# Softmax weights scaled on POOL ahead of P V, and an attention output kept with features on partitions

## The chip, the cores and the metric

One core of a Trainium2 chip runs the kernel. The metric is the device time of one execution in microseconds. The kernel before took 651.96 us as the median of 3 runs (651.56 to 653.12).

## The reference, cut to what matters

One decoder layer on 512 tokens of 1024 features, in float32. Two groups of eight heads with 64 output features each work side by side, and each group's output is normalised before a shared output projection:

```python
p = exp(s - m);  p = p / max(sum(p), 1e-30)          # masked softmax
y_mla = p_mla @ v                                    # 8 heads, causal
y_nsa = g0 * (p_c @ v_cmp) + g1 * (p_s @ v_slc) + g2 * (p_w @ v_win)   # g: sigmoid gates
mixed = concat(rmsnorm(y_mla, g_out_mla), rmsnorm(y_nsa, g_out_nsa))
h = h + mixed @ w_o
h = h + relu(rmsnorm(h) @ w_up) ** 2 @ w_down        # then a final rmsnorm
```

With 512 tokens, all 8 selected blocks are taken and the window is 512, so the selected branch and the window branch are both plain causal attention over four blocks of 128 tokens. The compressed branch attends to 31 (padded to 32) compressed keys.

## The kernel before, in words

A float32 operand that enters a matmul is split in two float32r parts, a high part (a rounded copy, by ACT) and a low part (the difference, by DVE); a product is the sum of two or three matmuls. Values V stand as a 128-column stationary tile: 64 columns of high parts beside 64 of low parts. So P V, with the transposed weights as the moving operand, comes out with features on partitions, 64 rows of the high product over 64 of the low one (`ot`, 128 x 512), and the two halves are still to be added.

The attention stretch is a pipeline of 24 units (`units`, L849): eight MLA heads (`unit_mla`, L654; one head, all four blocks of queries), then eight units of the selected branch and eight of the window and compressed branches (`unit_nsa`, L526, `br` 0 and 1; one block `i` of 128 queries and one group `g` of four heads, in the order of `ORDER`). Each unit has a stage of scores (score matmuls, a DVE operation that masks and finds the limit, an exponential on ACT that also sums) and a stage of P V (L574 on, and L687 on): transposes of the weights on TensorE, the split, two matmuls per block. In step `s` of the loop at L879 the scores of unit `s-1` and the P V of unit `s-2` advance in turn, and `fill` (L862) lets other work advance between the parts: projections that later units need, the compression MLP (`compressed`, L709) and the MLA half of the output projection (`out_mla`, L822). The tile framework then plans one order per engine by a simulated timeline, in which an instruction that stands earlier in the program goes first among those that are ready. Engines run their own queue strictly in order. The weights of a unit live in tiles `pr`, of which there are eight (two units' worth), and `load_wo` (L786) prepares the output weights, three of four times on POOL (`WOENG`, L28).

Behind P V, the kernel before does the following:

- MLA, and blocks 2 and 3 of the selected branch (`add_heads`, L631, `apart`): ACT copies `ot` to SBUF, TensorE transposes it back in four (L642), so that tokens are on partitions; DVE multiplies by the factor per token and head (L644), and POOL adds the halves (L646).
- Blocks 0 and 1 of the selected branch: four f32 matmuls with a folding matrix (`K_FOLD`, L649) transpose and add the halves at once; DVE multiplies (L651). An f32 matmul shows as two instructions in the trace.
- The window branch (L617 on): the same four folds (L623) and an f32 matmul of the transposed compressed weights (L577) with a block diagonal of the compressed values (`vbd`, L621) into one bank; DVE multiplies all by the factors (L626), POOL adds both products to y (L629).
- The factor is 1 / (sum x gate term), `weights_of` (L512): two small DVE operations.
- In units with more than one block, the first block's split goes through SBUF: ACT copies, DVE makes the high part (L591), POOL the low part (L592).
- y has tokens on partitions, so `norm_y` (L779) sums squares along rows on ACT, and `transpose_y` (L802) turns y by four transposes for each block of tokens and half (L805) before it is split and enters `out_proj` (L808).

Of the kernel before, what the change touches and what calls it, by code (L numbers as in the profile page):

```python
# [10 lines left out]
F32 = mybir.dt.float32  # L11
# [6 lines left out]
P = 128  # L18
# [6 lines left out]
APART = lambda br, i: br == -1 or br == 0 and i >= 2  # L25
LOP = lambda br, i, j: j == 0 and i > 0
# [11 lines left out]
DIRECT = lambda br, i: False  # L38
# [39 lines left out]
K_FOLD = 1185  # L78
K_END = 1249
# [15 lines left out]
def layer(ctx, tc, x, xt, w_in, w_uq, w_ukv, w1k, w2k, w1v, w2v, w_o, w_up, w_down, g_final, consts, vecs, out):  # L95
# [430 lines left out]
    def unit_nsa(i, g, br):  # L526
# [36 lines left out]
        if br == 1:  # L563
            nc.gpsimd.tensor_tensor(pc, pc, cm.unsqueeze(2).to_broadcast([P, 4, 32]), op=ALU.subtract)
            nc.scalar.activation(pc, pc, AF.Exp, scale=-1.0)
            if CSUM == "V":
                nc.vector.tensor_reduce(sums[:, 0:4], pc, axis=AX.X, op=ALU.add)
            else:
                half = m["wk2"].tile([P, 4, 16], F32, tag="half", name="half", bufs=2)
                nc.gpsimd.tensor_tensor(half, pc[:, :, 0:16], pc[:, :, 16:32], op=ALU.add)  # L570
                for n in (8, 4, 2):
                    nc.gpsimd.tensor_tensor(half[:, :, 0:n], half[:, :, 0:n], half[:, :, n:2 * n], op=ALU.add)
                nc.gpsimd.tensor_tensor(sums[:, 0:4], half[:, :, 0], half[:, :, 1], op=ALU.add)
        yield "ready"  # L574
# [5 lines left out]
        ot = bank(turn("ot", OT), "ot_ps")  # L580
        phs = []
        for j in range(i + 1):
# [12 lines left out]
            if not DIRECT(br, i):  # L595
                nc.tensor.matmul(ot, vc[:, 4 * j + brg, :], ph, start=(j == 0), stop=False)  # L596
                nc.tensor.matmul(ot, vc[:, 4 * j + brg, :], pl, start=False, stop=(j == i))
            phs.append((ph, pl))
            if j < i or not DIRECT(br, i):
                yield "part"  # L600
        if DIRECT(br, i):

            for h in range(4):
                hs = slice(h * P, (h + 1) * P)
                for j in range(i + 1):
                    for n in range(2):
                        nc.tensor.matmul(ot[:, hs], phs[j][n][:, hs], vc[:, 4 * j + brg, :],
                                         start=(j == 0 and n == 0), stop=(j == i and n == 1))
            yield "part"
        yv = m["yn"][:, i, 256 * g:256 * g + 256].rearrange("p (h d) -> p h d", h=4)  # L610
        gate = sg[:, i, :].rearrange("p (b n) -> p b n", b=3)[:, :, 4 * g:4 * g + 4]
        sv = sums.rearrange("p (b n) -> p b n", b=2)
        if br == 0:
            r = weights_of(sv[:, 1], gate[:, 1], "rg")
            add_heads(ot, r, yv, "direct" if DIRECT(br, i) else APART(br, i))
            return
        r = weights_of(sv, gate[:, 0:3:2], "rg")  # L617
        os_ = wk.tile([P, 512], F32, tag="os", name="os", bufs=2)
        nc.scalar.copy(os_, ot)
        b = bank(turn("ot", OT), "o_ps")  # L620
        nc.tensor.matmul(b[:, 0:256], pct, vbd[g], start=True, stop=True)  # L621
        for h in range(4):
            nc.tensor.matmul(b[:, 256 + 64 * h:320 + 64 * h], os_[:, h * P:(h + 1) * P], cst[:, K_FOLD:K_FOLD + 64],  # L623
                             start=True, stop=True)
        ow = m["wk2"].tile([P, 2, 4, 64], F32, tag="ow", name="ow", bufs=2)
        nc.vector.tensor_tensor(ow.rearrange("p b h d -> p (b h) d"), b.rearrange("p (h d) -> p h d", h=8),  # L626
                                r.rearrange("p b n -> p (b n)").unsqueeze(2).to_broadcast([P, 8, 64]), op=ALU.mult)
        for n in range(2):
            nc.gpsimd.tensor_tensor(yv, yv, ow[:, n], op=ALU.add)  # L629

    def add_heads(ot, r, yv, apart):  # L631

        if apart == "direct":
            b = ot
        else:
            os_ = wk.tile([P, 512], F32, tag="os", name="os", bufs=2)
            nc.scalar.copy(os_, ot)
            b = bank(turn("ot", OT), "o_ps")
        if apart:
            for h in range(4):  # L640
                if apart != "direct":
                    nc.tensor.transpose(b[:, h * P:(h + 1) * P], os_[:, h * P:(h + 1) * P], ident)  # L642
            oa = wk.tile([P, 4, 2, 64], F32, tag="oa", name="oa", bufs=1)
            nc.vector.tensor_tensor(oa.rearrange("p h a d -> p h (a d)"), b.rearrange("p (h n) -> p h n", h=4),  # L644
# [615 lines left out]
```

## Time and profile before

| | |
|---|---|
| median of 3 runs | 651.96 us |
| the profiled execution, its time and its span | 652.88 us, 651.0 us |
| busy: TensorE matmuls, weight loads | 635.2 us (98%), 571.5 us (88%) |
| busy: DVE, ACT, POOL | 429.9 us (66%), 336.6 us (52%), 240.0 us (37%) |
| mean granted clock of TensorE | 0.997 |

Busy time is the union of an engine's instructions. Matmuls overlap in the array and their ends are modelled, so a matmul of 512 columns shows some 390 ns while the next one starts after some 230; the chain of waits counts each piece only as far as it delays the next. The part from 309 us to the end of the span is the MLP.

### The profile page before, as it was taken

Reading aid. Unit: us, or ns where it says so; the run is one execution under the profiler, and the core shown is the slowest. Engines: PE = TensorE matmul, PEld = TensorE weight load, DVE = VectorE, ACT = ScalarE, POOL = GpSimd, SP = SyncE. Lnnn points to the kernel's source line nnn. Section 1 sums busy time; section 2 is a strip of 40 time slices with the busy share of each in tenths; the row PEclk is TensorE's granted clock in tenths of the full one; section 3 lists DMA queues with packets and bytes.
Section 4 is the critical chain, followed back from the end, with each engine's and each line's share of the span. In section 5 each row is a group of like instructions: output and inputs, shape, how many; then the busy total and the mean of one; then the engine's idle time right before and its main releaser. Section 6 shows DMA issues by size and latency. Waiting matters only on the chain.

```text
span 651.0 us, 10981 instructions
## 1 busy us (share of the span) xinstructions
PE 635.2 (98%) x4092; PEld 571.5 (88%) x4092; DVE 429.9 (66%) x898; ACT 336.6 (52%) x702; POOL 240.0 (37%) x294
## 2 busy tenths in 40 slices
PE   7999999999999999999999999999999999999996
PEld 5989999998878888889998889988899988999885
DVE  5767577856788589768967435794259843497425
ACT  5567677857946478732884115541144521355213
POOL 3864402235783139613110225413154231344031
PEclk9999999999999999999999999999999999999998
DMA  6533210105322101063135313254122541124003
GB/s 193 154 99 82 68 50 17 33 2 195 99 78 88 33 2 33 1 216 108 46 116 163 98 33 98 88 171 131 33 81 63 181 140 55 63 68 147 15 2 129
DMA packets 47125, 56.53 MB, mean 87 GB/s; under 512 B 4320, under 2 KB 34784, under 8 KB 47072
## 3 DMA queue, kind: packets, MB, share of 16 engines
q1 hardware_dynamic: 46784, 55.57, 27.9%
q8 instruction: 32, 0.52, 0.3%
q10 hardware_dynamic: 288, 0.26, 0.1%
q14 instruction: 21, 0.17, 0.1%
HBM read 53.72 MB, written 2.10 MB: 86 GB/s over the span
## 4 chain that ended last, share of the span: by engine, by line
PE 86%; DVE 5%; DMA 3%; ACT 2%; POOL 2%; issue 1%; SPq 1%; POOLq 0%; ACTq 0%; DVEq 0%
PE up_ps L990 25%; PE dn_ps L131 9%; PE dn_ps L132 9%; PE dn_ps L130 9%; PE wo_ps L130 2%; PE wo_ps L132 2%; PE wo_ps L131 2%; PE pt_ps L585 2%; PE hid_ps L730 2%; PE s_ps L547 1%; PE pt_ps L692 1%; PE ot_ps L596 1%; PE wq_ps L132 1%; PE wq_ps L131 1%; PE wq_ps L130 1%; PE s_ps L548 1%
## 5 line engine op out<-in xcount | busy, mean ns | idle before, releaser
L130 PE MATMUL dn_ps<-dw,ah 128*128 128x512 f32 (+1 forms) x264 | 101.9, 386 | 0.0
L131 PE MATMUL dn_ps<-dw,ah 128*128 128x512 f32 (+1 forms) x264 | 101.9, 386 | 0.0
L132 PE MATMUL dn_ps<-dw,al 128*128 128x512 f32 (+1 forms) x264 | 101.7, 386 | 0.0
L990 PE MATMUL up_ps<-ttT,uw 128*128 128x256 f32 x720 | 89.5, 282 | 0.4
L990 PEld LDWEIGHTS up_ps<-ttT,uw 128*128 128x128 f32 x720 | 87.2, 189 | 1.0 <-ACT snap L1019 1.0
L990 PE MATMUL up_ps<-ttB,uw 128*128 128x256 f32 x648 | 82.0, 282 | 0.0
L990 PEld LDWEIGHTS up_ps<-ttB,uw 128*128 128x128 f32 x648 | 79.6, 189 | 0.5
L958 POOL TENSOR_TENSOR us<-us,ur 128x1024 f32<-128x1024 f32 x14 | 41.4, 2958 | 101.2 <-DVE uw L125 101.2
L958 POOL TENSOR_TENSOR us<-ur 128x1024 f32<-128x1024 f32 x14 | 35.3, 2530 | 99.8 <-DMA ur<-in_w_up 49.7
L125 DVE TENSOR_TENSOR uw<-us,uw 128x1024 fp32r<-128x1024 f32 x28 | 37.4, 1336 | 47.2 <-ACT uw L111 47.2
L125 DVE TENSOR_TENSOR dw<-dr,dw 128x1024 fp32r<-128x1024 f32 x32 | 43.8, 1368 | 35.3 <-ACT dw L111 35.3
L131 PEld LDWEIGHTS dn_ps<-dw,ah 128*128 128x128 f32 x264 | 49.6, 188 | 10.6
L130 PEld LDWEIGHTS dn_ps<-dw,ah 128*128 128x128 f32 x264 | 49.6, 188 | 10.5
L132 PEld LDWEIGHTS dn_ps<-dw,al 128*128 128x128 f32 x264 | 49.5, 188 | 10.6
L111 ACT CAST uw<-us 128x1024 fp32r<-128x1024 f32 x28 | 29.4, 1049 | 55.5 <-PE dn_ps L132 40.7
L125 DVE TENSOR_TENSOR uw<-ur,uw 128x1024 fp32r<-128x1024 f32 x25 | 39.5, 1582 | 25.6 <-ACT uw L111 25.6
L111 ACT CAST dw<-dr 128x1024 fp32r<-128x1024 f32 x32 | 33.2, 1048 | 38.0 <-PE dn_ps L132 21.5
L111 ACT CAST uw<-ur 128x1024 fp32r<-128x1024 f32 x25 | 26.2, 1049 | 29.9 <-PE dn_ps L132 26.7
L560 ACT ACTIVATE pr<-pr,mx 128x256 f32<-128x256 f32 (+3 forms) x64 | 36.0, 565 | 6.9 <-DVE mx L552 5.2
L125 DVE TENSOR_TENSOR pl<-pt_ps,ph 128x512 fp32r<-128x512 f32 (+3 forms) x60 | 34.2, 577 | 8.2 <-ACT ph L111 6.9
L111 ACT CAST ph<-pt_ps 128x512 fp32r<-128x512 f32 (+3 forms) x60 | 29.7, 499 | 15.5 <-PE pt_ps L585 5.4
L1156 DVE SCALAR_TENSOR_TENSOR xs<-dn_ps,small,xs 128x512 f32<-128x512 f32 (+1 forms) x33 | 23.0, 734 | 19.9 <-PE dn_ps L132 19.9
(326 smaller groups left out, 1533.5 us busy)
## 6 DMA issues: line engine op xcount, KB each, us to landing
ur<-in_w_up SPq DMA_DIRECT2D x32, 512.0 KB, 3.9
dr<-in_w_down SPq DMA_DIRECT2D x32, 512.0 KB, 3.8
wor<-in_w_o SPq DMA_DIRECT2D x16, 256.0 KB, 3.1
wqraw<-in_w_in SPq DMA_DIRECT2D x16, 128.0 KB, 2.2
xs<-in_x SPq DMA_DIRECT2D x4, 512.0 KB, 5.4
wmraw<-in_w_in SPq DMA_DIRECT2D x8, 208.0 KB, 4.3
xr<-in_xt SPq DMA_DIRECT2D x3, 512.0 KB, 3.8
out<-xs SPq DMA_DIRECT2D x6, 256.0 KB, 2.2
```

Of the source, the lines that this page charges most:

```text
L111: nc.scalar.copy(dst, src)
L125: (lo_eng or nc.vector).tensor_tensor(lo, src, hi.bitcast(F32), op=ALU.subtract)
L130: nc.tensor.matmul(o, a_hi, b_hi, start=first, stop=False)
L131: nc.tensor.matmul(o, a_hi, b_lo, start=False, stop=False)
L132: nc.tensor.matmul(o, a_lo, b_hi, start=False, stop=last)
L547: nc.tensor.matmul(S[:, :b - a], qs, ka[:, brg, a:b], start=True, stop=False)
L560: nc.scalar.activation(pr[:, :L], pr[:, :L], AF.Exp, bias=lim, scale=-1.0, accum_out=sums[:, 4 + h:5 + h])
L585: nc.tensor.transpose(b[:, h * P:(h + 1) * P], prs[h][:, j * P:(j + 1) * P], ident)
L730: nc.tensor.matmul(hp[0:96, 0:P], xx[:, 2 * i:2 * i + 16 * 95 + 1:16], w1[:, j, :], start=(i == 0), stop=(i == 15))
L958: add = lambda o, x, y: nc.gpsimd.tensor_tensor(o, x, y, op=ALU.add)
L990: nc.tensor.matmul(oj, v[:, x, k, s], t[:, y, k, :], start=first and j == 0 and k == 0 and n == 0, stop=k == 3 and n == 2, skip_group_chec ...
L1156: nc.vector.scalar_tensor_tensor(xs[:, t, cs], accs[t, a][:, a:b], r4[:, t:t + 1], xs[:, t, cs], op0=ALU.mult, op1=ALU.add)
```

## The change

The scores stage now ends with the factors: `weights_of` and one POOL multiplication per weight tile, in place, before P V (`scaled`). The product is then final up to the sum of its halves, which DVE adds straight out of PSUM into a y that has features on partitions (`halves`). The compressed weights are scaled too, transposed head by head, split, and accumulated by two matmuls in the same bank. The fold matrix, the block diagonal, the transposes back, those of y, and the detour of the first block through SBUF go. Per block of tokens and half, `turned` splits y and makes the sum of squares: a square on ACT, two halving adds on POOL, and a matmul with ones.

```diff
-    vbd = [nsa.tile([P, 256], F32, name=f"vbd{g}") for g in range(2)]
+    vcc = [nsa.tile([32, P], R32, name=f"vcc{g}") for g in range(2)]
-    ym = yp.tile([P, NT, 512], F32, name="ym")
+    ymT = yp.tile([P, 4, T], F32, name="ymT")
 # unit_nsa, end of the scores stage
+        if br == 0:
+            r = weights_of(sv[:, 1], gate[:, 1], "rg")
+        else:
+            rr = weights_of(sv, gate[:, 0:3:2], "rg")
+            r = rr[:, 1]
+            nc.gpsimd.tensor_tensor(pc, pc, rr[:, 0].unsqueeze(2).to_broadcast([P, 4, 32]), op=ALU.mult)
+        scaled([(prs[h][:, :L], r[:, h:h + 1]) for h in range(4)])
         yield "ready"
+        ot = bank(turn("ot", OT), "ot_ps")
         if br == 1:
             b = bank(turn("pt", PT), "pct_ps")
-            nc.tensor.transpose(b[:, 0:P], pc.rearrange("p h n -> p (h n)"), ident)
-            pct = m["wk2"].tile([P, P], F32, tag="pct", name="pct", bufs=2)
-            nc.scalar.copy(pct, b[:, 0:P])
+            for h in range(4):
+                nc.tensor.transpose(b[0:32, h * P:(h + 1) * P], pc[:, h, :], ident)
...
+            split(pch, pcl, b[0:32, :])
+            nc.tensor.matmul(ot, vcc[g], pch, start=True, stop=False)
+            nc.tensor.matmul(ot, vcc[g], pcl, start=False, stop=False)
...
-            if LOP(br, i, j):
-                pb = m["wk2"].tile([P, 512], F32, tag="pb", name="pb", bufs=2)
-                nc.scalar.copy(pb, b)
-                nc.vector.tensor_copy(ph, pb)
-                nc.gpsimd.tensor_tensor(pl, pb, ph.bitcast(F32), op=ALU.subtract)
-            else:
-                split(ph, pl, b)
+            split(ph, pl, b)
...
+        halves(ot, ynT[:, 2 * g:2 * g + 2, i * P:(i + 1) * P], br == 1)
+        if br == 1 and g == 1:
+            turned(1, ynT, i)
+
+    def scaled(todo):
+        for p, r in todo:
+            nc.gpsimd.tensor_scalar(p, p, r, 1.0, op0=ALU.mult, op1=ALU.mult)
+
+    def halves(ot, y, more):
         os_ = wk.tile([P, 512], F32, tag="os", name="os", bufs=2)
...
+        nc.scalar.copy(os_[0:64], ot[64:128, :])
+        o = y
+        if more:
+            o = m["wk2"].tile([P, 2, P], F32, tag="y1", name="y1", bufs=2)
+        va, vb = (v.rearrange("p (a b n) -> p a b n", a=2, b=2) for v in (ot, os_))
+        for e in range(2):
+            nc.vector.tensor_tensor(o[64 * e:64 * e + 64], va[0:64, :, e], vb[0:64, :, e], op=ALU.add)
+        if more:
+            nc.gpsimd.tensor_tensor(y, y, o, op=ALU.add)
 # unit_mla, end of the scores stage
-            yield "part" if i < NT - 1 else "ready"
+            if i < NT - 1:
+                yield "part"
+        r = weights_of(sums[:, 0:4], None, "rm")
+        scaled([(prs[i][:, :(i + 1) * P], r[:, i:i + 1]) for i in range(NT)])
+        yield "ready"
 # unit_mla, end
-        r = weights_of(sums[:, 0:4], None, "rm")
-        add_heads(ot, r, ym[:, :, 64 * h:64 * h + 64], APART(-1, h))
+        nc.scalar.copy(os_[0:64], ot[64:128, :])
+        s = slice(64 * (h % 2), 64 * (h % 2) + 64)
+        nc.vector.tensor_tensor(ymT[s, h // 2, :], ot[0:64, :], os_[0:64], op=ALU.add)
 # in place of norm_y and transpose_y
+    def turned(part, y, t):
+        s = slice(t * P, (t + 1) * P)
+        split(m["yth"][:, :, s], m["ytl"][:, :, s], y[:, :, s])
+        jy = m["wo"].tile([P, 4, P], F32, tag="wor", name="jy", bufs=2)
+        nc.scalar.activation(jy, y[:, :, s], AF.Square)
+        for n in (2, 1):
+            nc.gpsimd.tensor_tensor(jy[:, 0:n], jy[:, 0:n], jy[:, n:2 * n], op=ALU.add)
+        b = bank("F" if part == 0 else "W", "ss_ps")
+        nc.tensor.matmul(b[:, 0:1], jy[:, 0, :], small[:, 76:77], start=True, stop=True)
+        rsqrt_mean(ry[:, 4 * part + t:4 * part + t + 1], b[:, 0:1], 512)
```

## Rows read from the trace of the kernel before

**Rows 1.** Chain of waits, whole span: share by engine.

```profile
PE 86%; DVE 5%; DMA 3%; ACT 2%; POOL 2%; issue 1%; SPq 1%; POOLq 0%; ACTq 0%; DVEq 0%
```

**Rows 2.** Table by stretch: length; PE, PEld, DVE, ACT, POOL busy us; clock; DMA share, GB/s.

```profile
76.00:156.00 80.00, 79.53 (x605) 76.22 (x603) 55.73 (x171) 56.76 (x159) 21.42 (x69) 1.00 0.18 57
156.00:228.00 72.00, 69.72 (x421) 60.18 (x419) 53.34 (x163) 46.03 (x126) 38.04 (x47) 1.00 0.24 72
228.00:278.00 50.00, 49.45 (x318) 41.44 (x317) 43.88 (x200) 38.93 (x110) 31.35 (x41) 1.00 0.04 12
278.00:309.00 31.00, 31.00 (x180) 26.84 (x179) 24.27 (x27) 8.81 (x11) 7.71 (x5) 1.00 0.55 170
```

**Rows 3.** Chain in order of time: start us, us, what (MLA, then window branch).

```profile
121.24 0.44 PE o_ps L642 x4
...
234.36 0.84 PE o_ps L623 x8
...
237.22 0.43 PE o_ps L621 x2
...
241.49 0.23 PE wo_ps L131
```

**Rows 4.** POOL by line and shape: busy us, mean ns, then idle before.

```profile
L592 POOL TENSOR_TENSOR pl<-pb,ph 128x512 fp32r<-128x512 f32 x12 | 15.4, 1285 | 4.9 <-DVE ph L591 4.9
...
L629 POOL TENSOR_TENSOR yn<-yn,ow 128x256 f32<-128x256 f32 x16 | 11.8, 736 | 6.3 <-DVE ow L626 6.0
...
L115 POOL TENSOR_SCALAR woh<-wor 128x512 fp32r<-128x512 f32 x12 | 7.5, 640 | 2.0 <-PE wo_ps L132 2.0
...
L646 POOL TENSOR_TENSOR ym<-oa 128x256 f32<-128x256 f32 x8 | 6.2, 776 | 1.2 <-DVE rg L519 1.2
...
L115 POOL TENSOR_SCALAR qs<-qf 128x256 fp32r<-128x256 f32 x8 | 3.2, 405 | 3.3 <-PE qt_ps L297 3.0
```

**Rows 5.** DVE by line and shape, 76 to 310 us.

```profile
L125 DVE TENSOR_TENSOR pl<-pt_ps,ph 128x512 fp32r<-128x512 f32 x36 | 24.6, 683 | 6.2 <-ACT ph L111 5.4 <-PE ot_ps L597 0.4
...
L591 DVE CAST ph<-pb 128x512 fp32r<-128x512 f32 x12 | 5.9, 495 | 1.2 <-ACT pb L590 1.1
...
L651 DVE TENSOR_TENSOR yn<-o_ps,rg 128x256 f32<-128x256 f32 x4 | 1.6, 405 | 0.4 <-PE o_ps L649 0.3
```

**Rows 6.** Timeline of ACT: last sum of a unit's exponentials (start us, us).

```profile
125.69 0.20 ACT L683 ACTIVATION_READ_ACCUMULATOR pr<-pr,mx 128x1 f32 x1
...
163.69 0.20 ACT L560 ACTIVATION_READ_ACCUMULATOR pr<-pr,mx 128x1 f32 x1
...
231.11 0.19 ACT L560 ACTIVATION_READ_ACCUMULATOR pr<-pr,mx 128x1 f32 x1
```

**Rows 7.** Timeline of TensorE: first transposes of the same three units.

```profile
134.56 0.49 PE L692 MATMUL pt_ps<-cst,pr 128*128 128x128 f32 x3
...
161.75 0.38 PE L585 MATMUL pt_ps<-cst,pr 128*128 128x128 f32 x2
...
232.33 0.60 PE L585 MATMUL pt_ps<-cst,pr 128*128 128x128 f32 x4
```

**Rows 8.** Timeline of POOL, selected branch.

```profile
161.13 1.37 POOL L798 TENSOR_SCALAR wor<-wor,vec 128x512 f32<-128x512 f32 x2
...
163.63 2.54 POOL L125 TENSOR_TENSOR wol<-wor,woh 128x512 fp32r<-128x512 f32 x2
...
187.12 1.28 POOL L592 TENSOR_TENSOR pl<-pb,ph 128x512 fp32r<-128x512 f32 x1
```

**Rows 9.** Timeline of DVE, selected branch.

```profile
185.68 0.31 DVE L744 TENSOR_TENSOR gw<-z 128x64 f32<-128x64 f32 x1
...
187.25 1.24 DVE L746 TENSOR_TENSOR gw<-gw,z 128x64 f32<-128x64 f32 x1
188.41 0.15 DVE L518 SCALAR_TENSOR_TENSOR rg<-sums,sg 128x4 f32<-128x4 f32 x1
188.59 0.18 DVE L519 RECIPROCAL rg<-rg 128x4 f32<-128x4 f32 x1
```

More of the change, by code (lines that the diff above doesn't have):

```diff
@@ L598, in unit_nsa @@
[L598 to L608, printed above, removed]
-            yield "part"
@@ L619, in unit_nsa @@
[L619 to L644, printed above, removed]
-                                    r.unsqueeze(2).to_broadcast([P, 4, P]), op=ALU.mult)
-            nc.gpsimd.tensor_tensor(yv, oa[:, :, 0, :], oa[:, :, 1, :], op=ALU.add)
-            return
-        for h in range(4):
-            nc.tensor.matmul(b[:, 64 * h:64 * h + 64], os_[:, h * P:(h + 1) * P], cst[:, K_FOLD:K_FOLD + 64],
-                             start=True, stop=True)
-        nc.vector.tensor_tensor(yv, b[:, 0:256].rearrange("p (h d) -> p h d", h=4), r.unsqueeze(2).to_broadcast([P, 4, 64]),
-                                op=ALU.mult)
@@ new lines, in unit_nsa @@
+            split(ph, pl, b)
+            nc.tensor.matmul(ot, vc[:, 4 * j + brg, :], ph, start=(j == 0 and br == 0), stop=False)
+            nc.tensor.matmul(ot, vc[:, 4 * j + brg, :], pl, start=False, stop=(j == i))
+            yield "part"
+        halves(ot, ynT[:, 2 * g:2 * g + 2, i * P:(i + 1) * P], br == 1)
[4 more added lines that the diff above has]
+            nc.gpsimd.tensor_scalar(p, p, r, 1.0, op0=ALU.mult, op1=ALU.mult)
@@ L770, in compressed @@
             for g in range(2):
-                nc.gpsimd.memset(vbd[g], 0.0)
-                for h in range(4):
-                    nc.vector.tensor_copy(vbd[g][32 * h:32 * h + 32, 64 * h:64 * h + 64], kc[32 * g:32 * g + 32, 0, :])
+                split(vcc[g][:, 0:64], vcc[g][:, 64:128], kc[32 * g:32 * g + 32, 0, :])
     ny, ry = col(40, 8), col(48, 8)
     sh, r4 = col(56, 8), col(64)
-    def norm_y(y, part):
-        for t in range(NT):
-            jy = m["wo"].tile([P, 4, P], F32, tag="wor", name="jy", bufs=2).rearrange("p a b -> p (a b)")
-            at = 4 * part + t
-            nc.scalar.activation(jy, y[:, t], AF.Square, accum_out=ny[:, at:at + 1])
-            rsqrt_mean(ry[:, at:at + 1], ny[:, at:at + 1], 512)
+    def turned(part, y, t):
[8 more added lines that the diff above has]
+        rsqrt_mean(ry[:, 4 * part + t:4 * part + t + 1], b[:, 0:1], 512)
     def load_wo(part, vcol, c, eng, lo_eng=None):
@@ L800, in load_wo @@
         return h, l
-    def transpose_y(y, t, yh, yl, tag):
-        b = bank(tag, "yt_ps")
-        for k in range(4):
-            nc.tensor.transpose(b[:, k * P:(k + 1) * P], y[:, t, k * P:(k + 1) * P], ident)
-        split(yh, yl, b)
     def out_proj(part, t, c, w, yh, yl, tag, every=4):
@@ L840, in out_mla @@
                 yield
-            yield from out_proj(0, t, c, w[c], m["yth"][:, t], m["ytl"][:, t], "F", 1)
+            yield from out_proj(0, t, c, w[c], m["yth"], m["ytl"], "F", 1)
             yield
@@ L888, in layer @@
             wk2 = m["wk2"] = tc.alloc_tile_pool(name="wk2", **reuse)
-            yn = m["yn"] = wk2.tile([P, NT, 512], F32, name="yn")
+            ynT = wk2.tile([P, 4, T], F32, name="ynT")
             late = ctx.enter_context(tc.tile_pool(name="late", side="right", **reuse))
@@ L907, in layer @@
             whole(f[3])
-    norm_y(yn, 1)
     w, yth, ytl = (m[n] for n in ("won", "yth", "ytl"))
-    for t in range(NT):
-        transpose_y(yn, t, yth[:, t], ytl[:, t], "B")
     wk2.release()
```

35 lines of the change are left out of this document (10 added, 25 removed).

## The prediction

> **What bounds the kernel now.** I read the page's chain of waits first, then a table of busy time by stretch, then the chain in order of time for prices, then POOL and DVE by shape, and last short timelines for order. The chain lies on TensorE for 86% of the span [rows 1]. The table [rows 2] splits what the change touches into four stretches: MLA (76 to 156 us), the selected branch (156 to 228), the window branch (228 to 278) and the tail (278 to 309); behind 309 nothing is edited. TensorE's matmuls are busy 79.5 of 80, 69.7 of 72, 49.5 of 50 and 31.0 of 31 us, at a granted clock of 1.00, the 2.4 GHz level. So TensorE time that is taken out should come off the span, unless another engine is late in its place. The one near it is DVE in the window stretch: 43.9 of 50 us.
>
> **What leaves and enters TensorE.** Prices are from the chain, which counts a piece as it delays the next: four transposes 0.44 us, eight fold instructions (four f32 matmuls) 0.84, the two for `vbd` 0.43, one 512-column matmul 0.23 [rows 3].
> Removed: 8 MLA units x 0.44 = 3.5; the selected branch 4 folds x 0.84 + 4 x 0.44 = 5.1; the window branch 8 x (0.84 + 0.43 + 0.11 for the transposed `pc`) = 11.0; the transposes of y 8 x 0.44 = 3.5. Together 23.1.
> Added: in each of 8 window units four transposes and two 512-column matmuls, 0.44 + 0.46 = 0.90, so 7.2; and 8 one-column f32 matmuls for the square sums, two instructions each. These cost between nothing (a gap takes them) and the fold's 0.105 an instruction; I take the latter, 1.7, since the fold is the nearest f32 form. Together 8.9.
> Net 14.2 us less: MLA 3.5, selected 5.1 + 1.8 - 0.9 = 6.0 (half of the y transposes run there), window 11.0 - 7.2 - 0.6 = 3.2, tail 1.5. That nothing is actually removed can be excluded: each of these is a line that the diff deletes.
>
> **What enters POOL.** It has single-input rows of 0.64 us at 512 columns and 0.405 at 256 [rows 4]; on that line 128 columns cost 0.29 and 384 cost 0.52. An MLA unit has one tile of each width, 1.85; an attention unit of 1 to 4 blocks has four equal tiles: 1.2, 1.6, 2.1 or 2.6. Both branches run each size twice: 8 x 1.85 + 4 x 7.5 = 45 us. Added too are the compressed weights' multiply (8 x 0.37, half of the 256-column add of 0.74), the add of the window output to y (8 x 0.74) and two halving adds of squares per row of tokens (8 x 1.1): 18 us. Removed are 12 subtractions of 1.29, 16 adds of 0.74 and 12 of 0.78: 37 us [rows 4]. POOL gets 26 us more. It has room: 21.4 of 80, 38.0 of 72 and 31.4 of 50 us are busy [rows 2]. Its total is no bound; its place is. The scaling stands between the last exponential and the first transpose of a unit, and all four tiles must be done.
>
> **How late that is.** Behind the last exponential come two small DVE operations (0.15 + 0.18, [rows 9]) and the four scalings.
> - MLA: the exponential ends at 125.9 and the transposes start at 134.6 [rows 6, 7]. 8.7 us of slack against 0.35 + 1.85: hidden. Only the first unit has no such lead; I give 0.5 back.
> - Selected: the transposes begin at 161.75 while the last exponential ends at 163.9. They would come 2.1 + 0.35 + 1.6 = 4.1 us later. POOL is in addition closed from 161.1 to 166.2 by output weights [rows 8], so 6.3 us at worst. What is queued behind a waiting scaling on POOL are those weights' own operations and the `pow` of the norm; PV waits for the scaling. Two units beside it start as early. The cost is between zero (scores of the next unit and `hid` matmuls take the gap) and 3 x 4.1 + 2.2 = 14.5 us. I take 2.5: the later units of this stretch have TensorE work waiting for any gap, the first ones little.
> - Window: 231.3 to 232.3, a gap of 1.0 us against 0.35 + 1.2. Small for this unit, but the units grow.
>
> **What enters DVE.** `halves` replaces one PSUM operation by two of 256 columns at 0.405 [rows 5]; the split of the compressed weights brings one of 512 columns at 0.68. In the window branch a unit has 2 x 0.405 + 0.68 - 0.68 = 0.81 more: 6.5 us. The low parts come back from POOL: six times 0.68 for 0.50, 1.1 us. Three of the y splits (0.68) move in from the tail: 2.0. DVE would want 43.9 + 9.6 = 53.5 us in a stretch for which TensorE, after its saving, wants 46.8. In MLA one 512-column operation replaces another: nothing; in the selected branch 3 to 4 us more fit into 72 - 53.3 = 19. ACT gets eight 512-column copies for 128-column ones; it has 38.9 of 50 us busy in the window stretch, so I cost that at nothing while DVE stands ahead of it.
> How much of the window saving is lost lies between nothing (early scores are read before 228 and the splits of y slip behind 278) and 53.5 - 46.8 = 6.7. I take 5.0, near the upper end, as that end is a sum of measured rows and the lower needs work to move.
>
> First the row: in the window stretch weight loads are busy 41.4 of 50 us, DVE 43.9, matmuls 49.5 [rows 2]. The Trainium skill, Perfetto Trace Analysis, section Identifying the Most-Contended Engine, says that matmul busy time is a poor measure and that weight-load share should be taken for TensorE. By that rule DVE is the busier engine there and sets the stretch: all 6.7 go back, and the sum is 1.7 us higher than mine. By the matmul row none goes back.
>
> **The sum.** -14.2 + 0.5 + 2.5 + 5.0 = -6.2 us. The profiled execution took 652.88 us (span 651.0), 0.9 above the median of 651.96. 652.88 - 6.2 = 646.7; as a median 645.8, say **646**. About 0.3%, 2 us, is what a measurement of this kernel tells from no change, so 650 to 654 counts as the same.
>
> **Rivals.**
> 1. All is hidden. The order is planned again for the new work, so plan and queues can absorb the waits. For: the MLA slack, and POOL with over a third free in every stretch now. Against: DVE's 53.5 us. 652.88 - 14.2 - 0.9 gives 637.8.
> 2. Slower: the scaling becomes what PV waits for in each attention unit. Place: between the last exponential and the first transpose, on POOL. Price: 14.5 us for three selected units, and for the eight window units 0.35 + 1.9 (mean of the four sizes) less the gap of 1.0, 8 x 1.25 = 10; 24.5 in all. It decides when over 14.2 of these, 58%, reach TensorE. At 80% it is 19.6 - 14.2 = 5.4 slower: 657. For: transposes start within 1 us of the exponential or before it. Against: out projections and the next unit's scores stand ready in most places.
> A row that adds to this: a 64-column DVE multiply took 1.24 us, from 187.25, while POOL ran a subtraction from 187.12 to 188.40; its neighbour of the same size took 0.31 [rows 8, 9]. The Trainium skill, GPSIMD Engine Reference, section Specifications, says that POOL's SBUF interface is shared with DVE instructions that have two SBUF inputs. The trace agrees. By that rule the first of the two operations that make the factor, which reads sums and gates, can wait for one scaling (0.64): up to 16 x 0.5 = 8 us more on the same place, at most.
> 3. A draw: the waits give back 10 to 16 us, half of rival 2 and most of DVE's excess: 652.
>
> **Chances.** Forecast (641 to 650): 0.46. All hidden: 0.17. Draw: 0.18. Slower: 0.19. So faster 0.63, same 0.18, slower 0.19. The range leaves out half of rival 1 and half of rival 2: 638.5 to 655.5; the forecast's own is 641 to 650.
>
> **What would show it.** Right: in the table by stretch MLA ends some 3 us earlier and keeps matmuls busy; the selected stretch is 3 to 4 us shorter with a wait of the transposes for POOL near its start; the window stretch is about 52 us with DVE over 90% busy; no fold or y transposes in the list by line. Wrong: the window stretch at 47 us (DVE did not bind), or POOL as the releaser of the transposes in most units and a longer selected stretch (rival 2). If the part behind 309 changes by over 1 us, something that I left out, such as the order of the weight loads, is at work.

## The result and the profile after

| | before | after |
|---|---|---|
| median | 651.87 us (4 runs) | 679.51 us (4 runs, 678.94 to 681.08) |
| ratio, 95% interval | | 1.0424 [1.0401, 1.0447] |
| profiled execution: time, span | 652.88, 651.0 us | 679.93, 678.1 us |
| mean granted clock of TensorE | 0.997 | 0.970 |

The change costs 27.6 us. The table by stretch of the changed kernel answers to [rows 2], with the same columns; its last two stretches are longer because P V ends later.

```profile
76.00:156.00 80.00, 77.58 (x584) 73.56 (x583) 57.92 (x177) 60.14 (x164) 35.06 (x97) 1.00 0.18 57
156.00:228.00 72.00, 67.32 (x348) 54.92 (x346) 51.40 (x155) 42.25 (x107) 44.56 (x69) 0.95 0.20 63
228.00:278.00 50.00, 45.36 (x183) 30.62 (x181) 36.66 (x167) 31.58 (x89) 25.84 (x50) 0.76 0.05 16
278.00:310.00 32.00, 27.81 (x126) 19.75 (x125) 20.07 (x53) 13.12 (x27) 17.72 (x27) 0.89 0.28 91
310.00:340.00 30.00, 27.45 (x176) 24.56 (x176) 24.13 (x27) 10.69 (x12) 9.12 (x6) 1.00 0.28 89
```

Two things are new. TensorE's matmuls leave 18.5 us of these 264 idle, where the rows of before leave 3.3 of 233. And the granted clock is no longer 1.00: 0.95, 0.76 and 0.89. A clock column of 0.76 over 50 us means that 24 us of them were at the 1.2 GHz level. Weight by length: 0.05 x 72 + 0.24 x 50 + 0.11 x 32 = 19 us of full-speed time are missing. The span grew by 27.1 us, and the last P V matmul moved by 34.9 (four of the output projections that followed it now run ahead of it). These are its rows, before and after:

```profile
L597 PE MATMUL ot_ps<-pl,vc x40: 387/398/502, 160.5 to 274.9; 128*128 128x512 f32 x40
```

```profile
L598 PE MATMUL ot_ps<-pl,vc x40: 392/482/775, 163.5 to 309.8; 128*128 128x512 f32 x40
```

(ns least, median, longest; first and last start in us.) What TensorE waits for, in the list of waits of its weight loads in the changed kernel, 150 to 310 us (sum in us, times, longest):

```profile
PEld s_ps L543 <- DVE mx L548: 7.7, 12, 2.4
PEld ot_ps L598 <- DVE pl L121: 6.9, 11, 2.6
PEld pct_ps L584 <- POOL pc L577: 2.9, 2, 1.6
PEld qt_ps L293 <- ACT qt L294: 2.8, 2, 1.9
PEld pt_ps L593 <- POOL pr L607: 2.6, 10, 0.5
```

POOL's scaling (L607) is the releaser for 2.6 us in all, ten short waits. By this list it looks harmless; most waits are put down to DVE. The timelines show better what happened. Here is the second attention unit of the changed kernel, from its last exponential to its first transposes, on ACT, DVE, POOL and TensorE in turn:

```profile
161.63 0.21 ACT L556 ACTIVATION_READ_ACCUMULATOR pr<-pr,mx 128x1 f32 x1
...
161.01 1.16 DVE L121 TENSOR_TENSOR ytl<-ymT,yth 128x512 fp32r<-128x512 f32 x1
...
163.64 0.68 DVE L121 TENSOR_TENSOR ytl<-ymT,yth 128x512 fp32r<-128x512 f32 x1
164.24 0.68 DVE L121 TENSOR_TENSOR pl<-pt_ps,ph 128x512 fp32r<-128x512 f32 x1
164.84 0.28 DVE L514 SCALAR_TENSOR_TENSOR rg<-sums,sg 128x4 f32<-128x4 f32 x1
...
166.84 0.17 DVE L515 RECIPROCAL rg<-rg 128x4 f32<-128x4 f32 x1
...
159.91 3.38 POOL L121 TENSOR_TENSOR wol<-wor,woh 128x512 fp32r<-128x512 f32 x2
...
167.18 1.85 POOL L607 TENSOR_SCALAR pr<-pr,rg 128x256 f32<-128x256 f32 x4 [2.07 <-DVE rg L515]
...
170.16 1.04 PE L593 MATMUL pt_ps<-cst,pr 128*128 128x128 f32 x8
```

The exponentials are done at 161.84. The two operations that make the factor last 0.45 us together, but DVE is an in-order queue: they stand behind splits and the next unit's scores and are done at 167.0, 5.2 us later. Then come 1.85 us of scaling, and the transposes start 8.3 us behind the last exponential (the last 1.1 us are TensorE's own queue: sixteen matmuls of the compression MLP stand ahead). In the kernel before, the same unit started its transposes 2.1 us ahead of it [rows 6, 7].

Not every wait of this stretch is the scaling's. TensorE's two longest ones near it are for ACT's copies of the queries and for DVE's first operation on the scores (L548), which stands behind the split of 1.16 us above:

```profile
153.37 0.53 PE L293 MATMUL qt_ps<-idr,qs 128*128 128x128 f32 x4 [1.74 <-ACT qt L294]
...
162.69 0.69 PE L543 MATMUL s_ps<-ka,qt 128*128 128x384 f32 x1 [1.98 <-DVE mx L548]
```

The clock falls to 0.50 behind each of them (156 to 159 and 163 to 166 us), the first time before any scaling was waited for.

### The profile page after: what moved, and what is told of

It reads as the page before. It is cut to its first block, busy times and chain, and to the rows that moved or that the text cites. A ratio compares the mean times of both kernels' runs of the same rounds, so it can differ in the third digit from the quotient of the medians.

```text
span 678.1 us, 10873 instructions
## 1 busy us (share of the span) xinstructions
PE 647.3 (95%) x3956; PEld 567.2 (84%) x3956; DVE 440.3 (65%) x916; ACT 342.8 (51%) x696; POOL 273.8 (40%) x380
## 4 chain that ended last, share of the span: by engine, by line
PE 82%; DVE 7%; issue 3%; DMA 3%; ACT 2%; POOL 2%; SPq 1%; POOLq 0%; ACTq 0%; DVEq 0%
PE up_ps L957 24%; PE dn_ps L127 8%; PE dn_ps L128 8%; PE dn_ps L126 8%; PE pt_ps L593 3%; PE wo_ps L126 2%; PE wo_ps L127 2%; PE wo_ps L128 2%; PE hid_ps L705 1%; PE ot_ps L598 1%; PE s_ps L543 1%; DVE pr L548 1%; PE pt_ps L665 1%; PE ot_ps L597 1%; PE wq_ps L127 1%
## 5 line engine op out<-in xcount | busy, mean ns | idle before, releaser
L121 DVE TENSOR_TENSOR uw<-us,uw 128x1024 fp32r<-128x1024 f32 x28 | 38.5, 1376 | 45.6 <-ACT uw L107 45.6
L121 DVE TENSOR_TENSOR dw<-dr,dw 128x1024 fp32r<-128x1024 f32 x32 | 43.7, 1366 | 35.0 <-ACT dw L107 35.0
L121 DVE TENSOR_TENSOR uw<-ur,uw 128x1024 fp32r<-128x1024 f32 x25 | 37.7, 1508 | 27.7 <-ACT uw L107 27.7
L107 ACT CAST ph<-pt_ps 128x512 fp32r<-128x512 f32 (+1 forms) x72 | 36.0, 515 | 32.5 <-PE pt_ps L593 26.8
L121 DVE TENSOR_TENSOR pl<-pt_ps,ph 128x512 fp32r<-128x512 f32 (+1 forms) x72 | 41.9, 595 | 12.9 <-ACT ph L107 12.5
L607 POOL TENSOR_SCALAR pr<-pr,rg 128x256 f32<-128x256 f32 (+3 forms) x64 | 33.6, 543 | 22.6 <-DVE gw L723 17.4
L556 ACT ACTIVATE pr<-pr,mx 128x256 f32<-128x256 f32 (+3 forms) x64 | 35.7, 559 | 13.6 <-DVE mx L548 13.4
```

The lines of the kernel that those rows point to most:

```text
L107: nc.scalar.copy(dst, src)
L121: (lo_eng or nc.vector).tensor_tensor(lo, src, hi.bitcast(F32), op=ALU.subtract)
L556: nc.scalar.activation(pr[:, :L], pr[:, :L], AF.Exp, bias=lim, scale=-1.0, accum_out=sums[:, 4 + h:5 + h])
L607: nc.gpsimd.tensor_scalar(p, p, r, 1.0, op0=ALU.mult, op1=ALU.mult)
```

## The experiments

Three theories. **Theory 1**: the factor (DVE) and the scaling (POOL) between last exponential and transposes are longer than the one turn that lies there; TensorE runs dry and its clock falls. **Theory 2**: the compressed weights, now at the head of P V, are late. **Theory 3**: DVE has too much to do.

Every edit makes the framework plan the order of all engines anew. By the traces about a third of DVE's instructions run in another order in e1 and in e8 than in the changed kernel, about a tenth in e3. What a new plan is worth by itself was not measured, so differences of two or three us below are no proof of a cause.

### One cost at a time

**e1**: the multiplications of the weight tiles left out.

```diff
-            nc.gpsimd.tensor_scalar(p, p, r, 1.0, op0=ALU.mult, op1=ALU.mult)
+            pass
```

> The POOL multiplications of the weight tiles are left out (the factors are still made, the compressed weights are still scaled, y is not normalised by the sums of the main branches). Theory 1 (the wait for POOL's scaling between the last exponential and the transposes is what lets TensorE run dry and its clock fall): of the 27.6 us that the change costs at least 15 go, 650 to 664 us, and the stretches at 1.2 GHz between 230 and 300 us shrink to below 10 us. Theory 2 (the compressed weights, now at the head of P V, are what is late) and theory 3 (more DVE work in the window branch): within 5 us of the changed kernel's 679.5, since neither the compressed path nor DVE's queue is touched.

666.1 us, 1.0214 [1.0187, 1.0242]: 13.4 of the 27.6 us come back, less than the 15 that theory 1 asked for. In the selected branch P V then waits for no factor, so both prices are out there; in the window branch the compressed weights at the head of P V still wait for theirs. The edit also takes POOL's work from beside DVE. It is half of the cost, no more. Its stretches:

```profile
156.00:228.00 72.00, 67.37 (x363) 55.78 (x362) 55.43 (x181) 45.60 (x122) 29.00 (x39) 0.95 0.21 64
228.00:278.00 50.00, 45.52 (x216) 32.60 (x217) 43.59 (x184) 35.93 (x94) 25.66 (x40) 0.93 0.23 74
278.00:309.00 31.00, 27.91 (x137) 21.30 (x136) 17.94 (x28) 10.78 (x16) 5.91 (x8) 0.94 0.16 48
```

The matmuls' idle time in 228 to 278 is the same as in the changed kernel (4.5 against 4.6 us); what came back there is the clock, 0.93 for 0.76. In the selected branch the clock did not come back (0.95 in both).

**e2**: the compressed product moved behind the last block of P V, in the same accumulation.

```diff
+            if j < i or br == 0:
+                yield "part"
         if br == 1:
             b = bank(turn("pt", PT), "pct_ps")
...
+            nc.tensor.matmul(ot, vcc[g], pch, start=False, stop=False)
+            nc.tensor.matmul(ot, vcc[g], pcl, start=False, stop=True)
```

> The transposes, the split and the two matmuls of the compressed weights stand behind the last block of P V instead of ahead of the first, in the same bank. Theory 2 (compressed weights at the head of P V): the window branch no longer waits for them, at least 8 us go, below 672 us. Theory 1 (POOL's scaling): within 4 us of 679.5, since the first transposes still wait for the scaling. Theory 3 (DVE work): the same.

677.0 us, 1.0381 [1.0360, 1.0402]: 2.5 us. Theory 2 falls as a main cause.

**e5**: 128 rows instead of 32 in the compressed product, the lower ones zero.

```diff
-    vcc = [nsa.tile([32, P], R32, name=f"vcc{g}") for g in range(2)]
+    vcc = [nsa.tile([P, P], R32, name=f"vcc{g}") for g in range(2)]
...
-            split(pch, pcl, b[0:32, :])
+            split(pch[0:32, :], pcl[0:32, :], b[0:32, :])
```

> The stationary tile and the moving operand of the compressed product get 128 rows, of which 96 are zero, in place of 32. In the trace of the changed kernel one of these 512-column matmuls holds TensorE for 0.43 us also at 2.4 GHz, where one with 128 rows holds it for 0.23. If it is the 32 rows that cost this, the pace falls to 0.23 and 16 x 0.2 = 3.2 us go at least (676), more if TensorE is then fed better. If it is something else (a wait that the trace does not show), the pace stays at 0.43 and the time within 1.5 us of 679.5.

674.2 us, 1.0339 [1.0316, 1.0362]: 5.3 us. The chain in order of time shows what a matmul of this product holds up, first in the changed kernel, at full clock:

```profile
305.04 0.43 PE ot_ps L588
305.47 0.59 PE pt_ps L593 x4
306.06 0.42 PE ot_ps L589
306.48 0.44 PE ot_ps L597
```

and with 128 rows:

```profile
245.24 0.23 PE ot_ps L588
245.47 0.23 PE ot_ps L596
...
250.12 0.23 PE ot_ps L587
250.35 0.24 PE ot_ps L597
```

The piece behind a 32-row matmul is longer too: 0.59 us for four transposes that cost 0.44 elsewhere in this chain, 0.44 for a 128-row matmul that costs 0.23. By these pieces each of the 16 costs 0.35 to 0.4 us more, 5.6 to 6.4 us together (an estimate); the run gave 5.3.

**e4**: the kernel before with the MLA part of the change alone.

```diff
+        r = weights_of(sums[:, 0:4], None, "rm")
+        scaled([(prs[i][:, :(i + 1) * P], r[:, i:i + 1]) for i in range(NT)])
         yield "ready"
...
-        add_heads(ot, r, ym[:, :, 64 * h:64 * h + 64], APART(-1, h))
+        nc.vector.tensor_tensor(ymT[s, h // 2, :], ot[0:64, :], os_[0:64], op=ALU.add)
```

> The kernel before with the MLA part of the change alone: weights scaled on POOL, no transposes back, features on partitions up to the output projection, sums of squares by a matmul with ones for that half. By the working of the prediction this part saves 3.5 + 1.8 - 0.9 = 4.4 us on TensorE and gives 0.5 back: 648 us. Theory 1 in a strong form (any unit that waits for POOL's scaling loses): 652 or more.

653.2 us (10 runs), 1.0018 [1.0007, 1.0030]: no gain and no loss worth the name. That lies in theory 1's strong form (652 or more), but not for its reason: TensorE's waits from 76 to 156 us name POOL neither here nor in the changed kernel. TensorE's work did go:

```profile
76.00:156.00 80.00, 78.94 (x591) 73.97 (x590) 58.07 (x178) 61.26 (x166) 34.56 (x94) 1.00 0.18 57
156.00:228.00 72.00, 69.84 (x412) 59.79 (x411) 53.87 (x175) 45.82 (x126) 43.11 (x54) 1.00 0.22 71
228.00:278.00 50.00, 47.00 (x298) 40.05 (x299) 41.77 (x180) 35.84 (x97) 32.12 (x41) 1.00 0.04 12
```

P V of the first selected unit starts 3.8 us earlier than before (151.4 for 155.2), but in the window branch the matmuls are now idle 3.0 of 50 us where they were idle 0.6 [rows 2], and the last P V matmul starts at 273.7 for 274.9: by these rows the time taken out earlier comes back as idle time there.

### The clock, the distance, the factor

**e3**: the changed kernel with four more small matmuls on zeros after each turn's part of the window branch (136 in all, their results unused).

```diff
+DUM = 4
...
+        if s >= 18:
+            wb = bank("W", "warm_ps")
+            for n in range(DUM):
+                nc.tensor.matmul(wb[:, 0:P], zr, zr, start=True, stop=True)
```

> The changed kernel with four small additional matmuls (128 columns of bf16, their results unused) after each turn's part in the window branch, some 33 times. Their own cost by the nearest row (a 128-column matmul takes 0.06 to 0.11 us here) is 8 to 14 us if TensorE never waits there. If the lower clock itself is a cause (30.7 us at half clock in the window branch, worth up to 15 us) and the additional work keeps the clock up: 665 to 676, and the granted clock of the window branch is 0.95 or more. If the stalls are the cause and the low clock only lies where TensorE waits anyway: 680 or more.

671.7 us, 1.0291 [1.0268, 1.0314]: more work for TensorE made the kernel 7.8 us faster. The window branch in steps of 12 us, the changed kernel first, e3 second:

```profile
228.00:240.00 12.00, 10.09 (x43) 6.56 (x42) 9.14 (x56) 8.60 (x32) 4.77 (x13) 0.76 0.00 1
240.00:252.00 12.00, 10.68 (x33) 6.86 (x31) 7.12 (x30) 6.42 (x17) 6.14 (x12) 0.50 0.01 1
252.00:264.00 12.00, 12.00 (x48) 8.65 (x47) 8.46 (x34) 6.14 (x16) 5.95 (x12) 0.74 0.07 22
```

```profile
228.00:240.00 12.00, 11.40 (x76) 8.36 (x77) 10.80 (x74) 11.05 (x39) 5.02 (x14) 1.00 0.01 1
240.00:252.00 12.00, 10.71 (x41) 7.14 (x40) 9.73 (x39) 7.73 (x21) 8.08 (x16) 0.72 0.01 1
252.00:264.00 12.00, 12.00 (x88) 9.10 (x88) 8.39 (x31) 7.37 (x20) 5.02 (x9) 1.00 0.08 24
```

In the changed kernel TensorE waits 0.58 and 1.02 us between 231 and 233.5 and then runs at 1.2 GHz from 234 to 258. "Busy" of 12.00 with 48 matmuls and of 12.00 with 88 are different amounts of work. So the low clock is itself a cause; it does not just lie where TensorE waits anyway. How much of the 7.8 us is the clock's and how much the new plan's, this run does not tell apart.

**e8**: the changed kernel with P V of each selected and window unit three turns behind its scores instead of two (MLA stays at two; some small tiles get more buffers, one gets a buffer less).

```diff
-    NPR, NPH, NW = 8, 2, 8
+    NPR, NPH, NW = 12, 2, 8
...
-        stages = [live[s - d] for d in (1, 2) if 0 <= s - d < len(units)]
+        stages = [live[s - d] for d in (1, 2, 3) if 0 <= s - d < len(units) and (d == 1 or (d == 3) == (s - d >= 8))]
```

> The changed kernel whole, with P V of each NSA unit three turns behind its scores instead of two (twelve buffers for the weights instead of eight, one os buffer instead of two); no arithmetic is changed. Theory 1 (what comes between the last exponential and the first transposes of a unit, the factor on DVE and the scaling on POOL, is too long for the one turn that lies between, TensorE runs dry and its granted clock falls): a turn more covers it, under 660 us, and the stretch of NSA attention shows fewer than 10 us at the lower clock. Theory 3 (DVE has too much to do, and in its in-order queue the factors and the two additions stand ahead of the next scores): DVE's work is the same, so within 6 us of 679.5. Theory 2 (the compressed product at the head of P V) lies between, since its inputs too get a turn more, but its split stays on the path: 665 to 674.

661.2 us, 1.0127 [1.0110, 1.0144]: 18.3 us come back with all the arithmetic in place. Theory 3 said within 6 of 679.5, theory 1 under 660, which is missed by 1.2. The time at half clock did not go below theory 1's 10 us either: by the clock column it is some 15.

```profile
156.00:228.00 72.00, 66.64 (x365) 55.05 (x364) 54.22 (x183) 47.88 (x126) 46.87 (x75) 0.97 0.23 67
228.00:278.00 50.00, 46.93 (x227) 34.09 (x225) 40.94 (x178) 32.72 (x86) 38.54 (x65) 0.93 0.05 17
278.00:309.00 31.00, 28.37 (x145) 22.46 (x145) 20.89 (x31) 12.99 (x19) 6.90 (x9) 0.94 0.44 136
```

**e7**: no more buffers, P V begun two parts later within its turn.

```diff
+        wait = [live[s - 2]] if 0 <= s - 2 < len(units) else []
...
+            if turns == (2 if s >= 10 else 0) or not stages:
+                stages, wait = stages + wait, []
```

> The changed kernel whole, with the P V of an NSA unit begun two parts later within its turn (after the second of the four scores of the next unit), with no more buffers. Theory 1: the time between the last exponential and the first transposes grows by two parts, which is some 3 of the 6 to 10 us of a turn: 664 to 672, between the changed kernel (679.5) and P V a whole turn later (661.2). If it is only the order of work at a turn's head that matters: 661 to 664. If the distance does nothing and the buffers of the run with three turns were what helped: 677 to 682.

672.7 us, 1.0307 [1.0277, 1.0337]: 6.8 us, less distance and less gain, 0.7 us above the range that theory 1 gave and well below that of the buffers.

**e16**, the control: the kernel before with the same three turns (the edit of e8; to make room, two tiles share a buffer and some small ones have fewer).

> The kernel before, not changed but for P V of the NSA units three turns behind (and the buffers that this takes). If the 18 us that a turn more gave back in the changed kernel answer to the factor and the scaling, which the kernel before does not have ahead of P V: within 3 us of 652.7. If more distance is a gain in any kernel of this shape, and so says nothing of the scaling: 640 to 648.

655.2 us, 1.0053 [1.0037, 1.0069]: there the distance, with these smaller buffers, costs 3.3 us. The 18.3 us of e8 answer to the change's own wait.

**e17**: three turns and 128 rows, without the scaling.

> The run with P V three turns behind and 128 rows (660.2 us) without the scaling of the weight tiles on POOL (the factors are computed, the output is not normalised). If a turn more covers the scaling: 658 to 661. If the scaling is still waited for, or POOL's load still slows DVE: 655 or less; the part without distance was 13.4 us.

661.2 us, 1.0145 [1.0124, 1.0165], against 660.2 with it (e9 below): at this distance the scaling costs nothing, and POOL's work beside DVE nothing either. Theory 1 is shown from both sides for the larger part of the 27.6 us: take the scaling away or give it a turn, and its price is gone.

**e11**: the changed kernel without factors and scaling, and **e6**: without the scaling, with the edits of e2 and e5.

> The changed kernel without the factors at all: neither DVE's maximum and reciprocal nor any multiplication on POOL, so the output is not normalised; beside the run without the scaling alone (666.1 us) it takes 48 small DVE instructions and 8 multiplications of the compressed weights away. Theory 3 (DVE's in-order queue: these small instructions wait for the sums and hold up the scores behind them): 655 or less. Theory 1: the scaling was the cost and is already away there, so 664 to 668. Theory 2 (compressed path): 8 multiplications by about 0.35 us sit ahead of the compressed transposes, so 3 to 4 us less, 662 to 664.

> The changed kernel with three edits of single runs together: no scaling of the weight tiles (the output is not normalised), the compressed product behind the last block, and 128 rows in the compressed product. If the three costs simply add (13.4, 2.5 and 5.3 us by the single runs): 658. If they are one stall that is paid once, and any remaining late input keeps it: 663 to 666, as without the scaling alone. If nothing but these three is behind the loss, and the predicted TensorE saving of about 11 us comes through: 641 to 646.

663.8 us, 1.0171 [1.0131, 1.0211], and 663.9 us, 1.0172 [1.0152, 1.0192]. Beside e1, e11 is 2.3 us faster, but its two runs (661.7 and 666.0) overlap with those of e1 (665.0 and 667.3), so the small DVE operations have no price here; the three costs of single runs (13.4 + 2.5 + 5.3 = 21.2) come to 15.6 together, so much of them is one stall, paid once.

### What is left with the scaling covered

**e9**: e8 with the 128 rows of e5.

> The run with P V three turns behind (661.2 us) with 128 rows in the compressed product. In the changed kernel alone this gave 5.3 us. If TensorE's own work is what is left once the inputs come in time: 655 to 657. If what is left is DVE's queue and the lower clock: 659 to 662.

660.2 us, 1.0117 [1.0086, 1.0147], 1.0 us better than e8, which the spread of the runs does not tell from nothing: with TensorE waiting for others, its own work counts little. The next runs edit e9 to find the rest.

**e12**: four small matmuls per part from the third attention unit on (the edit of e3).

> The kernel before this one in the list, with four small additional matmuls after each turn's part from the third NSA unit on (some 60 times four; 106 of them took 6.1 us in the run with them in the window branch alone, so some 12 to 14 us here if TensorE never waits). If the lower clock still costs there (17 us at half clock with P V three turns behind, up to 8.5 us) and the waits take the additional work in: 650 to 656. If nothing of it is hidden: 660 to 668.

667.4 us, 1.0227 [1.0189, 1.0265]: now they cost 7.2 us (272 of them, twice as many as in e3). What helped at a clock of 0.5 is only work at one of 0.93 and more (e9's clock column: 0.93, 1.00 and 0.94).

**e13**: the low part of the first block by way of ACT and POOL again, as in the kernel before.

```diff
+            if j == 0 and i > 0:
+                nc.scalar.copy(pb, b)
+                nc.vector.tensor_copy(ph, pb)
+                nc.gpsimd.tensor_tensor(pl, pb, ph.bitcast(F32), op=ALU.subtract)
```

> The first kernel of this list, with the kernel before's way for the first block's low part (ACT copies the bank, DVE casts it from SBUF, POOL subtracts: rows of before 0.50 for 0.68 us on DVE, 1.285 us more on POOL, 12 times). Theory 3 (DVE's queue is what is left): DVE has 12 x 0.2 = 2.4 us less and waits on its results get shorter, 2 to 5 us faster than the first of the list. Without theory 3: the same within 2 us, or slower by what POOL's 15 us delay the scaling, up to 6 us.

675.0 us, 1.0342 [1.0312, 1.0372]: 14.7 us lost, more than either theory gave. The timelines of POOL, DVE and TensorE show what a fuller POOL does:

```profile
263.66 2.46 POOL L612 TENSOR_SCALAR pr<-pr,rg 128x384 f32<-128x384 f32 x4
266.08 0.62 POOL L111 TENSOR_SCALAR woh<-wor 128x512 fp32r<-128x512 f32 x1
266.67 1.27 POOL L121 TENSOR_TENSOR wol<-wor,woh 128x512 fp32r<-128x512 f32 x1
267.89 1.26 POOL L599 TENSOR_TENSOR pl<-pb,ph 128x512 fp32r<-128x512 f32 x1
269.11 1.26 POOL L121 TENSOR_TENSOR wol<-wor,woh 128x512 fp32r<-128x512 f32 x1
...
265.80 5.12 DVE L121 TENSOR_TENSOR ytl<-ynT,yth 128x512 fp32r<-128x512 f32 x1
...
271.59 0.60 PE L543 MATMUL s_ps<-ka,qt 128*128 128x272 f32 x1 [4.18 <-DVE mx L548]
```

A low part that P V needs (L599) stands behind 4.2 us of scaling and output weights. But the longest wait comes by another way: DVE's split of y takes 5.12 us here, where it takes 0.69 with POOL idle (at 292.95 in the same run), and ends only when POOL's run of operations has ended (270.37). DVE's operation on the next scores stands behind it, and TensorE waits 4.18 us for that. In all TensorE's matmuls wait 8.3 us for that operation of DVE (5.0 in e9) and 1.0 for low parts from POOL.

**e18**: the same without the scaling.

> The run with P V three turns behind, 128 rows and no scaling on POOL (661.2 us; the output is not normalised), with the kernel before's way for the first block's low part (a copy on ACT, a cast from SBUF on DVE, the subtraction on POOL) in 12 units. With the scaling on POOL this cost 14.7 us. If that was POOL's queue, now free: no loss any more, 657 to 662; and if DVE's work (theory 3) is what is left, the gain of 12 x 0.28 = 3.4 us of DVE shows: 655 to 658. If the way by POOL is itself late for P V: 666 or more.

661.6 us, 1.0128 [1.0089, 1.0166]: without the scaling on POOL nothing is lost, and the lighter DVE gains nothing either (661.2 in e17).

**e14**: the first output projection begun two turns later (`(10, len(units) + 3, ...` becomes `(12, ...`).

> The run with P V three turns behind and 128 rows (660.2 us), with the lane of the first output projection (its four splits of the turned output, 3.6 us of DVE and 4.7 us of ACT in the run before, stand ahead of the second NSA unit's factor) begun two turns later. If that burst at the head of the selected branch is what is left (10.2 us at half clock there, TensorE 5.5 us idle in 72): 650 to 655. If the saved TensorE work is simply not on the path any more and the burst only moves into the next units: 658 to 664.

667.2 us, 1.0237 [1.0220, 1.0254]: 7 us slower, past both expectations (five runs, 662.7 to 668.6). Moving the burst away from the head of the selected branch gave nothing back.

**e19**: `turned(1, ynT, t)` for all four rows behind the window branch.

> The run with P V three turns behind and 128 rows (660.2 us), with the split and the squares of the NSA output not in each turn of the window branch but behind the last, where the kernel before has them. If they are what holds up DVE and ACT in the window branch (4 x 0.68 us of DVE, 4 x 1.2 us of ACT): 655 to 658. If they are covered there: they then stand in front of the output projections with nothing beside them, 662 to 668.

663.6 us, 1.0159 [1.0113, 1.0206]: 3.4 us slower, so they are covered where the change put them.

**e20**: the low part of the compressed weights left out of the product (the cut shows it against e9).

```diff
-            split(pch[0:32, :], pcl[0:32, :], b[0:32, :])
+            nc.scalar.copy(pch[0:32, :], b[0:32, :])
-            nc.tensor.matmul(ot, vcc[g], pcl, start=False, stop=False)
```

> The run with P V three turns behind and 128 rows (660.2 us) without the low part of the compressed weights (left out of the product, so the compressed branch has less precision): DVE has 8 subtractions of 0.68 us fewer in the window branch, 5.4 us, and TensorE 8 matmuls of 0.3 us fewer, 2.5 us; no wait is added. In the window branch of that run DVE is busy 59.3 of 68.4 us, 0.87; the kernel before has 45.4 of 51.0 there, 0.89. Theory 3 (DVE at the share that it can reach there sets the pace): 5.4 / 0.87 = 6.2 us less, 653 to 655. If only TensorE's own work counts: 657 to 658.5. If neither does and what is left lies outside the window branch: 659 to 661.5.

658.2 us, 1.0085 [1.0069, 1.0102]: 2.0 us, what TensorE's own matmuls explain; 5.4 us less of DVE do not show. In the window branch theory 3 is not the rest either.

None of these versions beats the kernel before. What is left at three turns is 7.5 us (660.2 against 652.7), of which the distance by itself is 3.3 in the control. Where the saved TensorE time went can be read from its table. The last 342 us are alike in all three kernels; these rows are the stretch from 76 us up to them, before, in the changed kernel and in e9:

```profile
76.00:309.00 233.00, 229.69 (x1516) 204.68 (x1515) 177.22 (x558) 150.53 (x403) 98.52 (x161) 1.00 0.22 67
```

```profile
76.00:336.10 260.10, 241.62 (x1376) 199.51 (x1375) 186.32 (x572) 155.78 (x395) 132.31 (x247) 0.93 0.19 60
```

```profile
76.00:316.00 240.00, 222.30 (x1370) 191.02 (x1369) 184.44 (x572) 154.65 (x394) 133.15 (x248) 0.97 0.21 65
```

Length less idle time less what the clock takes is TensorE's work at full speed, an estimate: 229.7 us before, 260.1 - 18.5 - 19 = 222.6 in the changed kernel, and in e9 240 - 17.7 - 6.9 = 215.4 (0.07 x 72 + 0.06 x 31 by its stretches). So in e9 14.3 us of work are gone, but 14.4 us of idle time have come in their place, and the clock takes the 6.9 on top. Most of that idle time is not the scaling's: from 150 to 300 us e9's matmuls wait 5.0 us for DVE's operation on the scores, 2.6 for ACT's high part of y and 2.4 for ACT's copies of the queries. Whether these waits can be taken out of the way, and what the new plan of each edit is worth, **stays open**.

## Why the prediction was wrong

It said 646 us, range 638.5 to 655.5, and gave "slower" 0.19. It took 679.5.

- **The step that failed: "How late that is".** The prediction put "two small DVE operations (0.15 + 0.18)" behind the last exponential and priced the factor by its duration, 0.35 us. In the second selected unit it took 5.2, because it queues behind what DVE was given earlier. It looked at the queues on POOL and for what waits there, but not at the queue in front of the factor on DVE. Its give-back for the scaling was 0.5 + 2.5 = 3.0 us; the window branch, with its gap of 1.0 us, got no term at all. Leaving the scaling out gave 13.4 (e1), a turn more gave 18.3 (e8).
- **No term for the clock.** The sum has none, since all stretches of before stood at 1.00 [rows 2]. That row says what the clock was with TensorE always busy, not what it would be with waits. About 19 us of full-speed time are missing by the clock column, and added matmuls alone gave 7.8 us back (e3). By the Trainium skill, TensorE: Matmul & The Clock Gate, section HAM oscillation, a long wait for data between two bursts of matmuls brings the clock down, so that the next burst starts slow. The trace agrees that the clock fell in the middle of the kernel behind waits (0.50 from 240 to 252); the waits here were short, 0.58 and 1.02 us just ahead of the fall.
- **Rival 2 named the place, "between the last exponential and the first transpose, on POOL", and the sign.** Its price of 24.5 us was for waits alone and set against 14.2 us of saving that it took as sure; at 80% it gave 657. The waits it priced are real (e1, e8, e17), but a stall also costs clock. What it added for DVE beside POOL, one scaling of 0.64 us at a time, is not the limit: in e13 one split of DVE lost 4.4 us beside POOL.
- **TensorE's net of 14.2 us: right in e9, half of it in the changed kernel.** By the estimate above TensorE's work fell by 14.3 us in e9 and by some 7 in the changed kernel. The match in e9 is closer than the two digits of the clock column allow (0.005 over 240 us is 1.2), so to the tenth it is luck. The two 32-row matmuls of a window unit were priced at 0.23 each from a 128-row row [rows 3]; they hold TensorE for 0.43 and lengthen what follows, 5.6 to 6.4 us too little. With 128 rows the changed kernel gains 5.3 (e5), with the stall covered 1.0 (e9). "TensorE time that is taken out should come off the span" failed: idle time took its place.
- **MLA: half right.** Its transposes end earlier as said (the last unit's first ones at 145.7 for 149.3), and the scaling is hidden. But the first selected unit starts at 155.5 for 155.2: TensorE waits for ACT's copies of the queries, a bound that TensorE's work had hidden. Alone, the MLA part gives nothing (e4) where 3.9 us were expected (4.4 less 0.5).
- **Selected: wrong.** 3 to 4 us shorter were forecast; the first window unit's transposes start at 233.95 for 228.18, 5.8 us later.
- **Window: wrong for another reason than DVE.** "DVE over 90% busy" was the mark; it is busy 36.7 of 50 us. At three turns, lightening it gave nothing (e18) or no more than TensorE's share (e20). That DVE sets the stretch, by whichever share of TensorE it is held against, was not borne out: DVE itself came to wait, 5.5 us for ACT's high parts and 4.3 for TensorE's scores from 228 to 310.
- **Behind 309 us: right.** The last 342 us hold 335.3 us of matmuls, as before.

## What to carry to other kernels

A step that moves in front of a consumer costs its place in the in-order queue of the engine that runs it, not only its duration (5.2 us for 0.45 here): read from the timeline what stands ahead of it there, and give the pipeline a stage before moving anything onto the path. On a kernel whose TensorE hardly waits (3.3 of 233 us here) and stands at 2.4 GHz, price every stall with the clock that it can cost, and check which waits for other engines the removed TensorE work was covering before counting it as a gain.

## What the hardware showed beyond that

- Small additional matmuls made the kernel faster where the granted clock had been 0.50 to 0.76 (e3, 7.8 us), and slower by 7.2 us, with twice as many, where it was 0.93 and more (e12).
- A 512-column matmul with 32 rows among 128-row ones holds TensorE for 0.43 us at full clock, one with 128 rows for 0.23 (e5); the piece behind it is 0.15 to 0.21 us longer too. The Trainium skill, TensorE: Matmul & The Clock Gate, section Why this matters for your kernels, gives both the same time; here the measurement decides. The difference is about that of one weight load (0.18 us here); that the load is not hidden when the number of rows changes would fit, but was not shown.
- DVE's split of an SBUF tile (L121 `ytl` above) took 0.68 us alone (at 163.64 in the changed kernel) and can take longer while POOL runs: 1.16 at 161.01 there, and 5.12 in e13 beside five POOL operations in a row. It need not: at 248.37 in the changed kernel, beside POOL's scaling, it took 0.69.
